# Feed-forward input projections as seven products of quarters

## The chip, the cores and the metric

One core of one Trainium2 chip runs the kernel in one launch. The metric is the device time of an execution in microseconds (us). TensorE is called PE here, VectorE DVE, ScalarE ACT, GpSimd POOL and SyncE, which issues the transfers, SP.

## The reference

The input is 512 tokens of 1024 features, held as `h`. Two blocks follow one another, each of two layers. The change is in the first block's feed-forward, which runs twice in each of its two layers, four times in all:

```python
def swiglu_ffn(x, w_in, w_out):
    gate, up = jnp.split(x @ w_in, 2, axis=-1)
    return (jax.nn.silu(gate) * up) @ w_out
...
h = h + 0.5 * swiglu_ffn(rms_norm(h, ffn1_norm[l]), ffn1_w_in[l], ffn1_w_out[l])
```

`w_in` is 1024 x 5632 (2816 gate and 2816 up columns) and `w_out` 2816 x 1024. The rest of a layer (a mixer of two kinds of heads, attention to a memory of 256 rows) and the second block's layers stay as they are.

## The kernel before

Everything is kept with features on the 128 partitions and tokens along the free axis: `h` is eight tiles of 128 features x 512 tokens. Products are in float32 precision made from two rounded parts: each operand is split into `hi` (a cast on ACT) and `lo` (source minus `hi`, a subtraction on DVE), and `mm3` issues three matmuls for each product: hi by hi, hi by lo, lo by hi.

`weights` (line 239) brings a block of weights in half blocks of up to four 128-row slices of 256 columns: a transfer from SP's queue into `wr`, a cast on ACT into `wh` (line 254), a subtraction on DVE into `wl` (line 255), two buffers of each. `block_fm_steps` (line 271) multiplies one block of 256 columns: for each half block, for each of its two 128-column halves, for each 128-row slice, three matmuls with the weights stationary and 512 tokens moving. `dense_fm_steps` (line 305) does so for a list of blocks and hands each result of 128 x 512 to a function. Both can be advanced a few matmuls at a time.

The feed-forward, `ffn` (line 459), makes the two parts of the normalised input first (`norm`): `xh`, `xl` are parts of `h` times the gain, and the factor of each token, `R`, is multiplied in after the product. It goes through 22 blocks of 128 gate and 128 up columns in groups of 8, 8 and 6 (`FF_GROUPS`). Each block is two times 8 x 3 = 24 matmuls; its results go through DVE and ACT (`gg`, `ss`, `uu`, lines 471 to 474) and are split into `ah`, `al`. After a group its share of the output projection follows, in four blocks of 256 columns that are added to `h` at line 478. There are seven PSUM banks for products.

A planner settles the order of each engine's instructions before the run, by their place in the code; `high_priority(offset=n)` moves what is in it n instructions ahead in that order. Weights have a lead of 80 (`AHEAD`). On the chip each engine takes its instructions in the order so settled, and waits at each for what it needs.

Of the kernel before, what the change touches and what calls it, by code (L numbers as in the profile page):

```python
# [9 lines left out]
F32 = mybir.dt.float32  # L10
F32R = mybir.dt.float32r
I32 = mybir.dt.int32
BF16 = mybir.dt.bfloat16
AF = mybir.ActivationFunctionType
ALU = mybir.AluOpType
# [3 lines left out]
P = 128  # L19
D = 1024  # L20
S = 512
# [1 line left out]
MEM = 256  # L23
DEPTH = 2
FF = 2816
NFF = FF // P
FF_GROUPS = ((0, 8), (8, 16), (16, 22))
NEG = -1e30
GD = 128
XH = 4  # L30
# [76 lines left out]
def _chunks(w, cols):  # L107

    w = np.asarray(w)
    k = w.shape[0] // P  # L110
    return [np.ascontiguousarray(w[:, c].reshape(k, P, -1).transpose(1, 0, 2)).reshape(P, -1) for c in cols]


def _weights(a):

    r256 = lambda lo, hi: [np.arange(c, c + 256) for c in range(lo, hi, 256)]
    out = {}
    for l in range(DEPTH):
        for n in ("ffn1", "ffn2"):
            wi = a[n + "_w_in"][l]  # L120
            wo = a[n + "_w_out"][l]
            out[n + "_in", l] = _chunks(wi, [np.concatenate([np.arange(P) + P * j, np.arange(P) + P * j + FF]) for j in range(NFF)])
            blocks = []
            for lo, hi in FF_GROUPS:
                blocks += _chunks(wo[lo * P : hi * P], r256(0, D))
            out[n + "_out", l] = blocks
        wi = a["w_in"][l]
        z0, a0 = 3072, 3584
        za = [
            np.concatenate([np.arange(z0, z0 + 256), np.arange(a0, a0 + 4)]),  # L130
            np.concatenate([np.arange(z0 + 256, z0 + 512), np.arange(a0 + 4, a0 + 8)]),
        ]
        out["mix_z", l] = _chunks(wi, za)
        out["mix_gdn", l] = _chunks(wi, r256(1536, 3072))
        out["mix_qk", l] = _chunks(wi, r256(0, 1024))
        out["mix_v", l] = _chunks(wi, r256(1024, 1536))
        wo = a["w_out"][l]
        out["mix_out_g", l] = _chunks(wo[4 * P :], r256(0, D))
        out["mix_out_s", l] = _chunks(wo[: 4 * P], r256(0, D))
        out["x_k", l] = _chunks(a["xattn_w_kv"][l], r256(0, D))  # L140
        out["x_v", l] = _chunks(a["xattn_w_kv"][l], r256(D, 2 * D))
        out["x_q", l] = _chunks(a["xattn_w_q"][l], r256(0, D))
        out["x_o", l] = _chunks(a["xattn_w_o"][l], r256(0, D))
        wi = a["w_in_2"][l]
        f0, q0 = 2048, 2056
        qf = [
            np.concatenate([np.arange(q0, q0 + 256), np.arange(f0, f0 + 4)]),
            np.concatenate([np.arange(q0 + 256, q0 + 512), np.arange(f0 + 4, f0 + 8)]),
        ]
        out["s_qf", l] = _chunks(wi, qf)  # L150
        out["s_kb", l] = _chunks(wi, r256(2568, 3080))
        out["s_vb", l] = _chunks(wi, r256(3080, 3592))
        out["s_gb", l] = _chunks(wi, r256(3592, 4104))
        out["s_qa", l] = _chunks(wi, r256(0, 512))
        out["s_ka", l] = _chunks(wi, r256(512, 1024))
        out["s_va", l] = _chunks(wi, r256(1024, 1536))
        out["s_ga", l] = _chunks(wi, r256(1536, 2048))
        out["s_out_b", l] = _chunks(a["w_out_2"][l][4 * P :], r256(0, D))
        out["s_out_a", l] = _chunks(a["w_out_2"][l][: 4 * P], r256(0, D))
        out["s_ple", l] = _chunks(a["w_ple_2"][l], r256(0, D))  # L160
        out["s_gate", l] = _chunks(a["w_ple_gate_2"][l], r256(0, D))
    return out


class Builder:
    def __init__(self, ctx, tc, gain_cols, waps):
        self.tc, self.nc = tc, tc.nc
        self.ctx = ctx
        self.gc = gain_cols
        self.waps = waps  # L170
        pool = lambda name, bufs=1, **kw: ctx.enter_context(tc.tile_pool(name=name, bufs=bufs, **kw))
        self.cp = pool("const")
        self.hp = pool("h")
        self.xp = pool("x")
        self.wp = pool("w")
        self.sp = pool("small", bufs=4)
        self.dp = pool("dram", space=bass.MemoryType.DRAM)
        self.n = self.blocks = 0
        self.pending = []
        self.turn = False  # L180
        self.turn_bank = 'n'
# [52 lines left out]
    def g(self, name, l):  # L234
        lo, hi = self.gc[name, l]
        return self.gt[:, lo:hi]
# [194 lines left out]
    def parts(self, h, gain):  # L431

        xh = self.xp.tile([P, 8, S], F32R, name=self.uid("xh"), tag="xh")
        xl = self.xp.tile([P, 8, S], F32R, name=self.uid("xl"), tag="xl")
        for k in range(8):
            self.split(xh[:, k], xl[:, k], h[k], gain[:, k : k + 1])
        return xh, xl
# [21 lines left out]
    def ffn(self, h, l, name):  # L459
        nc = self.nc  # L460
        with self.scope(self.uid("ffn")) as ap, self.banks(d=7, n=1):
            xh, xl, rc, R = self.norm(h, self.g(name + "_norm", l))
            for gi, (lo, hi) in enumerate(FF_GROUPS):
                n = hi - lo
                ah = ap.tile([P, 8, S], F32R, name=self.uid("ah"), tag="ah", bufs=2)
                al = ap.tile([P, 8, S], F32R, name=self.uid("al"), tag="al", bufs=2)
                for j in range(lo, hi):
                    pg, pu = self.block_fm(name + "_in", l, j, 8, xh, xl)
                    t = lambda s, b=2: ap.tile([P, S], F32, name=self.uid(s), tag=s, bufs=b)
                    gg, ss, uu = t("gg"), t("ss"), t("uu")  # L470
                    nc.vector.tensor_tensor(out=gg, in0=pg, in1=R, op=ALU.mult)  # L471
                    nc.scalar.activation(out=ss, in_=gg, func=AF.Silu)  # L472
                    nc.vector.tensor_tensor(out=uu, in0=pu, in1=R, op=ALU.mult)  # L473
                    nc.vector.tensor_tensor(out=uu, in0=uu, in1=ss, op=ALU.mult)
                    self.split(ah[:, j - lo], al[:, j - lo], uu)

                def add(f, ps):
                    nc.vector.scalar_tensor_tensor(out=h[f % 8], in0=ps, scalar=0.5, in1=h[f % 8], op0=ALU.mult, op1=ALU.add)

                self.dense_fm(name + "_out", l, n, ah, al, add, chunks=range(4 * gi, 4 * gi + 4))  # L480
                if self.mem_c is None and gi == 1:
                    self.memory_stats(lambda shape, tag, bufs: ap.tile(shape, F32, name=self.uid(tag), tag=tag, bufs=bufs))

    def add_to(self, h):
        def add(f, ps):
# [964 lines left out]
def lay(a):  # L1450

    arrays = {"consts": _CONST, "gains": _lay_gains(a)}
    fm = lambda v: np.ascontiguousarray(np.asarray(v).T.reshape(-1, P, v.shape[0]).transpose(1, 0, 2)).reshape(P, -1)
    arrays["xT"] = fm(a["x"][0])
    arrays["memT"] = fm(a["mem"][0])
    for l in range(DEPTH):
        arrays[f"pT{l}"] = fm(a["p_2"][l, 0])
    arrays["pos"] = np.ascontiguousarray(np.asarray(a["positions_2"])[0].reshape(NT, P).T)
    index, flat = {}, {}
    for (name, l), blocks in _weights(a).items():  # L1460
        where = []
        for blk in blocks:
            rows = flat.setdefault(name, [])
            where.append((sum(r.size for r in rows), blk.shape[1]))
            rows.append(blk.reshape(-1))
        index[name, l] = where
    for name, rows in flat.items():
        arrays["w_" + name] = np.concatenate(rows)
    return arrays, index
# [26 lines left out]
```

## Time and profile before

| | |
|---|---|
| median of 3 runs | 3278.52 us (3275.07 to 3278.74) |
| the profiled execution | 3277.66 us, its span 3275.9 us |
| PE busy | 3223.6 us, 98% of the span |
| DVE busy | 1874.4 us, 57% |
| ACT busy | 1307.1 us, 40% |
| transfers | 88 GB/s on average |

The span runs from the first to the last instruction of the trace; the time of the execution has a little around it. An engine's busy time is the sum over its instructions with overlaps counted once. Matmuls overlap one another, so that the duration of one is longer than the distance from one to the next.

### The profile page before, as it was taken

To read this page: it belongs to the slowest core of one execution; us is meant where nothing else is said; L and a number is where in the kernel's file an instruction comes from. 1 tells how busy PE (TensorE), PEld (TensorE's weight loads), DVE (VectorE), ACT (ScalarE), POOL (GpSimd) and SP (SyncE) were. 2 spreads that over 40 slices of the span, in tenths; PEclk is the share of its full clock that TensorE was granted. 3 is DMA by queue.
4 is the path that set the end of the run, shared out by engine and by line. 5 is a ranking of instruction groups with operands and counts; after the bars stand their busy time and mean duration, and the time that the engine had idled before them with its cause. 6 is when DMAs were issued, how large, how long until landed. Compare 5 with 4: busy or idle time off the path is not lost. (4 is left out here: it accounts for less than half of the span.)

```text
span 3275.9 us, 44469 instructions
## 1 busy us (share of the span) xinstructions
PE 3223.6 (98%) x17928; PEld 2652.3 (81%) x17928; DVE 1874.4 (57%) x3404; ACT 1307.1 (40%) x2083; POOL 134.0 (4%) x182
## 2 busy tenths in 40 slices
PE   9999999989999999999999989999999999999999
PEld 7888877778888888888887868888888997789877
DVE  5344567776544435443557776553435667766675
ACT  4222442444432223222353255432223556545563
POOL 0000003220000000000001130000000000000000
PEclk9999999999999999999999999999999999999999
DMA  4323320323222233323321223223223322223223
GB/s 145 97 93 94 91 84 27 84 67 120 67 94 91 96 95 92 97 91 96 90 91 46 65 71 116 65 90 97 92 95 97 91 86 77 78 91 97 71 72 103
DMA packets 84397, 286.92 MB, mean 88 GB/s; under 512 B 9824, under 2 KB 13152, under 8 KB 84192
## 3 DMA queue, kind: packets, MB, share of 16 engines
q1 hardware_dynamic: 84192, 284.10, 28.3%
q8 instruction: 140, 2.29, 0.3%
q14 instruction: 65, 0.53, 0.1%
HBM read 269.38 MB, written 2.10 MB: 83 GB/s over the span
## 5 line engine op out<-in xcount | busy, mean ns | idle before, releaser
L255 DVE TENSOR_TENSOR wl<-wr,wh 128x1024 fp32r<-128x1024 f32 (+2 forms) x512 | 617.2, 1205 | 610.6 <-ACT wh L254 609.2
L254 ACT CAST wh<-wr 128x1024 fp32r<-128x1024 f32 (+2 forms) x512 | 526.9, 1029 | 1002.8 <-PE psd L261 914.1
L261 PE MATMUL psd<-xh,wh 128*128 128x512 f32 x2112 | 842.4, 399 | 8.1 <-ACT xh L384 8.1
L261 PE MATMUL psd<-xl,wh 128*128 128x512 f32 x2112 | 841.5, 398 | 0.0
L261 PE MATMUL psd<-xh,wl 128*128 128x512 f32 x2112 | 838.7, 397 | 0.0
L261 PEld LDWEIGHTS psd<-xh,wh 128*128 128x128 f32 x2112 | 397.2, 188 | 107.8 <-ACT xh L384 8.1
L261 PEld LDWEIGHTS psd<-xh,wl 128*128 128x128 f32 x2112 | 398.1, 188 | 93.5 <-issue 1.2
L261 PEld LDWEIGHTS psd<-xl,wh 128*128 128x128 f32 x2112 | 398.0, 188 | 90.5 <-DVE xl L385 0.3
L261 PE MATMUL psd<-wh,xh 128*128 128x256 f32 (+1 forms) x1024 | 291.7, 285 | 0.1
L261 PE MATMUL psd<-wh,xl 128*128 128x256 f32 (+1 forms) x1024 | 289.5, 283 | 1.2 <-DVE xl L385 1.1
L261 PE MATMUL psd<-wl,xh 128*128 128x256 f32 (+1 forms) x1024 | 288.7, 282 | 0.0
L261 PE MATMUL psd<-ah,wh 128*128 128x512 f32 x704 | 278.3, 395 | 0.0
L261 PE MATMUL psd<-ah,wl 128*128 128x512 f32 x704 | 277.6, 394 | 0.0
L261 PE MATMUL psd<-al,wh 128*128 128x512 f32 x704 | 277.4, 394 | 0.0
L261 PEld LDWEIGHTS psd<-wh,xl 128*128 128x128 f32 x1024 | 193.6, 189 | 1.6 <-DVE xl L385 1.6
L261 PEld LDWEIGHTS psd<-wh,xh 128*128 128x128 f32 x1024 | 193.8, 189 | 1.3 <-ACT xh L384 0.5
L261 PEld LDWEIGHTS psd<-wl,xh 128*128 128x128 f32 x1024 | 194.0, 190 | 0.9
L473 DVE TENSOR_TENSOR uu<-psd,R 128x512 f32<-128x512 f32 x88 | 60.8, 691 | 174.6 <-PE psd L261 174.6
L261 PEld LDWEIGHTS psd<-ah,wl 128*128 128x128 f32 x704 | 131.9, 187 | 32.6
L261 PEld LDWEIGHTS psd<-al,wh 128*128 128x128 f32 x704 | 132.0, 187 | 31.8
L261 PEld LDWEIGHTS psd<-ah,wh 128*128 128x128 f32 x704 | 132.0, 188 | 31.6
L472 ACT ACTIVATE ss<-gg 128x512 f32<-128x512 f32 x88 | 55.8, 634 | 222.9 <-DVE gg L471 222.9
(402 smaller groups left out, 4263.8 us busy)
## 6 DMA issues: line engine op xcount, KB each, us to landing
wr<-w_ffn_in_dram SPq DMA_DIRECT2D x176, 512.0 KB, 3.7
wr<-w_ffn_out_dram SPq DMA_DIRECT2D x64, 512.0 KB, 3.7
wr<-w_ffn_out_dram SPq DMA_DIRECT2D x32, 384.0 KB, 3.1
wr<-w_mix_gdn_dram SPq DMA_DIRECT2D x24, 512.0 KB, 3.8
B<-B SPq DMA_DIRECT2D x40, 256.0 KB, 3.0
wr<-w_mix_qk_dram SPq DMA_DIRECT2D x16, 512.0 KB, 3.8
wr<-w_x_k_dram SPq DMA_DIRECT2D x16, 512.0 KB, 3.8
wr<-w_x_v_dram SPq DMA_DIRECT2D x16, 512.0 KB, 3.8
```

Of the source, the lines that this page charges most:

```text
L254: nc.scalar.copy(hi, raw)
L255: (nc.gpsimd if name in ON_POOL else nc.vector).tensor_sub(lo, raw, hi.bitcast(F32))
L261: mm = lambda a, b, first, last: nc.tensor.matmul(ps, a, b, start=first, stop=last, skip_group_check=flip)
L472: nc.scalar.activation(out=ss, in_=gg, func=AF.Silu)
L473: nc.vector.tensor_tensor(out=uu, in0=pu, in1=R, op=ALU.mult)
```

## The change

The gate and up columns are taken in 11 units of 256 gate and 256 up columns, in groups of 3, 3, 3 and 2. The first two units of a stage are computed as before, gate block and up block after one another (`ffn_plain`). For the others (`ffn_seven_steps`) the tokens are halved (256 each), the 1024 input features are halved (four slices of 128 each), and the columns are gate and up: a product of 2 x 2 by 2 x 2 quarters, made of seven products instead of eight. Sums of the token quarters (`s1` to `s4`) are made once a stage (`seven_parts`), the last in the place of a quarter of `xh`, `xl` that is not needed any more. Sums of the weight quarters are made for every unit, and each of the seven weight operands is split into parts. A product is 2 x 4 x 3 = 24 matmuls of 256 columns. Products accumulate in four banks, two of them more than once after their first content was read; DVE combines them. Loads, sums and splits of a unit's weights are given a lead of 110.

The output blocks of a group, which followed it, are now advanced a step (3, 6 or 9 matmuls) after each product of the next group and two after every fourth; what is left is done at the end of that group, and the last group's blocks at the end.

```diff
--- before.py
+++ after.py
@@ -23,8 +23,11 @@
 MEM = 256
 DEPTH = 2
 FF = 2816
-NFF = FF // P
-FF_GROUPS = ((0, 8), (8, 16), (16, 22))
+HS = S // 2
+FF_UNITS = FF // 256
+FF_GROUPS = ((0, 3), (3, 6), (6, 9), (9, 11))
+FF_PLAIN = 2
+FF_AHEAD = 110
 NEG = -1e30
 GD = 128
 XH = 4
@@ -119,10 +122,10 @@
         for n in ("ffn1", "ffn2"):
             wi = a[n + "_w_in"][l]
             wo = a[n + "_w_out"][l]
-            out[n + "_in", l] = _chunks(wi, [np.concatenate([np.arange(P) + P * j, np.arange(P) + P * j + FF]) for j in range(NFF)])
+            out[n + "_in", l] = _chunks(wi, [256 * u + c + np.arange(256) for u in range(FF_UNITS) for c in (0, FF)])
             blocks = []
             for lo, hi in FF_GROUPS:
-                blocks += _chunks(wo[lo * P : hi * P], r256(0, D))
+                blocks += _chunks(wo[lo * 256 : hi * 256], r256(0, D))
             out[n + "_out", l] = blocks
         wi = a["w_in"][l]
         z0, a0 = 3072, 3584
@@ -162,6 +165,16 @@
     return out
 
 
+class Units:
+
+    def __init__(self, tiles):
+        self.tiles = tiles
+
+    def __getitem__(self, key):
+        return self.tiles[key[1] // 2][:, key[1] % 2]
+
 class Builder:
     def __init__(self, ctx, tc, gain_cols, waps):
         self.tc, self.nc = tc, tc.nc
@@ -459,27 +472,174 @@
     def ffn(self, h, l, name):
         nc = self.nc
         with self.scope(self.uid("ffn")) as ap, self.banks(d=7, n=1):
-            xh, xl, rc, R = self.norm(h, self.g(name + "_norm", l))
+            gain = self.g(name + "_norm", l)
+            xh, xl, rc, R = self.norm(h, gain)
+            t = lambda s, b=2: ap.tile([P, S], F32, name=self.uid(s), tag=s, bufs=b)
+            acts = {}
+            out, late = iter(()), None
+
+            def add(f, ps):
+                nc.vector.scalar_tensor_tensor(out=h[f % 8], in0=ps, scalar=0.5, in1=h[f % 8], op0=ALU.mult, op1=ALU.add)
+
             for gi, (lo, hi) in enumerate(FF_GROUPS):
-                n = hi - lo
-                ah = ap.tile([P, 8, S], F32R, name=self.uid("ah"), tag="ah", bufs=2)
-                al = ap.tile([P, 8, S], F32R, name=self.uid("al"), tag="al", bufs=2)
-                for j in range(lo, hi):
-                    pg, pu = self.block_fm(name + "_in", l, j, 8, xh, xl)
-                    t = lambda s, b=2: ap.tile([P, S], F32, name=self.uid(s), tag=s, bufs=b)
-                    gg, ss, uu = t("gg"), t("ss"), t("uu")
-                    nc.vector.tensor_tensor(out=gg, in0=pg, in1=R, op=ALU.mult)
-                    nc.scalar.activation(out=ss, in_=gg, func=AF.Silu)
-                    nc.vector.tensor_tensor(out=uu, in0=pu, in1=R, op=ALU.mult)
-                    nc.vector.tensor_tensor(out=uu, in0=uu, in1=ss, op=ALU.mult)
-                    self.split(ah[:, j - lo], al[:, j - lo], uu)
-
-                def add(f, ps):
-                    nc.vector.scalar_tensor_tensor(out=h[f % 8], in0=ps, scalar=0.5, in1=h[f % 8], op0=ALU.mult, op1=ALU.add)
-
-                self.dense_fm(name + "_out", l, n, ah, al, add, chunks=range(4 * gi, 4 * gi + 4))
+                turn = 0
+                for u in range(lo, hi):
+                    acts[u] = [ap.tile([P, 2, S], F32R, name=self.uid(s), tag=s, bufs=5) for s in ("ah", "al")]
+                    if u < FF_PLAIN:
+                        self.ffn_plain(name, l, u, xh, xl, R, t, acts[u])
+                        if u == 0:
+                            sums, late = self.seven_parts(ap, h, gain, xh, xl)
+                    else:
+                        if late:
+                            late()
+                            late = None
+                        for _ in self.ffn_seven_steps(name, l, u, ap, xh, xl, sums, R, t, acts[u]):
+                            turn += 1
+                            for _ in range(1 + (turn % 4 == 0)):
+                                next(out, None)
+                self.drain(out)
+                ah, al = (Units([acts[u][i] for u in range(lo, hi)]) for i in range(2))
+                out = self.dense_fm_steps(name + "_out", l, 2 * (hi - lo), ah, al, add, chunks=range(4 * gi, 4 * gi + 4))
                 if self.mem_c is None and gi == 1:
-                    self.memory_stats(lambda shape, tag, bufs: ap.tile(shape, F32, name=self.uid(tag), tag=tag, bufs=bufs))
+                    self.memory_stats(lambda shape, tag, bufs: ap.tile(shape, F32, name=self.uid(tag), tag="ss", bufs=2))
+            self.drain(out)
+
+    def ffn_plain(self, name, l, u, xh, xl, R, t, act):
+
+        nc = self.nc
+        ss = []
+        for ps in self.block_fm(name + "_in", l, 2 * u, 8, xh, xl):
+            gg = t("gg")
+            nc.vector.tensor_tensor(out=gg, in0=ps, in1=R, op=ALU.mult)
+            ss.append(t("ss"))
+            nc.scalar.activation(out=ss[-1], in_=gg, func=AF.Silu)
+        for i, ps in enumerate(self.block_fm(name + "_in", l, 2 * u + 1, 8, xh, xl)):
+            uu = t("uu")
+            nc.vector.tensor_tensor(out=uu, in0=ps, in1=R, op=ALU.mult)
+            nc.vector.tensor_tensor(out=uu, in0=uu, in1=ss[i], op=ALU.mult)
+            self.split(act[0][:, i], act[1][:, i], uu)
+
+    def seven_parts(self, ap, h, gain, xh, xl):
+
+        nc = self.nc
+        lo, hi = slice(0, HS), slice(HS, S)
+        T = lambda: ap.tile([P, 4, HS], F32, name=self.uid("sr"), tag="sr", bufs=6)
+        g = lambda k: gain[:, k : k + 1]
+        part = lambda s: [ap.tile([P, 4, HS], F32R, name=self.uid(s + i), tag=s + i) for i in "hl"]
+        s3, s1, q, s4 = T(), T(), T(), T()
+        stt = lambda o, a, k, op, b: nc.vector.scalar_tensor_tensor(out=o, in0=a, scalar=g(k), in1=b, op0=ALU.mult, op1=op)
+        for k in range(4):
+            nc.scalar.activation(out=s3[:, k], in_=h[k][:, hi], func=AF.Copy, scale=g(k))
+            nc.scalar.activation(out=s4[:, k], in_=h[k + 4][:, lo], func=AF.Copy, scale=g(k + 4))
+            stt(s1[:, k], h[k + 4][:, hi], k + 4, ALU.subtract, s3[:, k])
+            stt(q[:, k], h[k][:, lo], k, ALU.add, s1[:, k])
+            stt(s3[:, k], h[k][:, lo], k, ALU.subtract, s3[:, k])
+        out = {n: part(n) for n in ("s1", "s2", "s3")}
+        self.split(*out["s2"], q, -1.0)
+        self.split(*out["s3"], s3)
+        self.split(*out["s1"], s1)
+        nc.vector.tensor_tensor(out=s4, in0=q, in1=s4, op=ALU.subtract)
+        out["s4"] = [x[:, 0:4, hi] for x in (xh, xl)]
+        return out, lambda: self.split(*out["s4"], s4)
+
+    def ffn_seven_steps(self, name, l, u, ap, xh, xl, s, R, t, act):
+
+        nc = self.nc
+        toks = slice(0, HS), slice(HS, S)
+        A = lambda th, kh: [x[:, 4 * kh : 4 * kh + 4, toks[th]] for x in (xh, xl)]
+        ahead = lambda: self.tc.high_priority(offset=FF_AHEAD)
+        T = lambda: ap.tile([P, 4, 256], F32, name=self.uid("sr"), tag="sr", bufs=6)
+        v = lambda x: x.rearrange("p (j c) -> p j c", j=2)
+        Rh = [R[:, ts].unsqueeze(1).to_broadcast([P, 2, HS]) for ts in toks]
+        tt = lambda o, a, b, op=ALU.add: nc.vector.tensor_tensor(out=o, in0=a, in1=b, op=op)
+
+        def load(c, kh):
+            w = T()
+            nc.sync.dma_start(out=w, in_=self.waps(name + "_in", l, 2 * u + c).rearrange("p (k c) -> p k c", k=8)[:, 4 * kh : 4 * kh + 4])
+            return w
+
+        def parts(w):
+            x = [ap.tile([P, 4, 256], F32R, name=self.uid(n), tag=n, bufs=2) for n in ("sh", "sl")]
+            self.split(*x, w)
+            return x
+
+        def product(ps, w, x, first=True):
+            for j in range(2):
+                fs = slice(j * P, (j + 1) * P)
+                for k in range(4):
+                    start = first and j == 0 and k == 0
+                    for i, (a, b) in enumerate(((0, 0), (0, 1), (1, 0))):
+                        nc.tensor.matmul(ps[:, j], w[a][:, k, fs], x[b][:, k], start=start and i == 0, stop=k == 3 and i == 2, skip_group_check=True)
+
+        xt = lambda tag: v(self.xp.tile([P, S], F32, name=self.uid(tag), tag=tag, bufs=1))
+        a, b, c, d = (self.ps("d", [P, 2, HS]) for _ in range(4))
+        with ahead():
+            b11 = load(0, 0)
+            w = parts(b11)
+        product(a, w, A(0, 0))
+        m1 = xt("acc")
+        nc.scalar.copy(m1, a)
+        yield
+        with ahead():
+            b12 = load(1, 0)
+            p1 = T()
+            tt(p1, b11, b12)
+            b22 = load(1, 1)
+            p2 = T()
+            tt(p2, p1, b22)
+            w = parts(p2)
+        product(b, w, s["s2"])
+        V = xt("sq")
+        tt(V, m1, b)
+        yield
+        with ahead():
+            tt(b12, b12, b22)
+            w = parts(b12)
+        product(c, w, s["s3"])
+        x22 = v(t("uu"))
+        tt(x22, V, c)
+        yield
+        with ahead():
+            w = parts(p1)
+        product(d, w, s["s1"])
+        tt(x22, x22, d)
+        tt(x22, x22, Rh[1], ALU.mult)
+        yield
+        with ahead():
+            b21 = load(0, 1)
+            w = parts(b21)
+        product(a, w, A(0, 1), False)
+        gates = v(t("gg")), v(t("gg"))
+        ss = [v(t("ss")) for _ in range(2)]
+        tt(gates[0], a, Rh[0], ALU.mult)
+        nc.scalar.activation(out=ss[0], in_=gates[0], func=AF.Silu)
+        yield
+        with ahead():
+            tt(p2, p2, b21)
+            w = parts(p2)
+        product(c, w, A(1, 1), False)
+        tt(gates[1], V, c)
+        tt(gates[1], gates[1], Rh[1], ALU.mult)
+        nc.scalar.activation(out=ss[1], in_=gates[1], func=AF.Silu)
+        yield
+        with ahead():
+            w = parts(b22)
+        product(d, w, s["s4"], False)
+        x12 = v(t("uu"))
+        tt(x12, V, d)
+        tt(x12, x12, Rh[0], ALU.mult)
+        for th, x in ((1, x22), (0, x12)):
+            nc.vector.scalar_tensor_tensor(out=x, in0=x, scalar=-1.0, in1=ss[th], op0=ALU.mult, op1=ALU.mult)
+            self.split(*(y[:, :, toks[th]] for y in act), x)
+        yield
 
     def add_to(self, h):
         def add(f, ps):
```

## Rows read from the trace of the kernel before

**Rows 1.** The page's busy times by engine and, in 40 slices, PE's busy share and granted clock.
```profile
PE 3223.6 (98%) x17928; PEld 2652.3 (81%) x17928; DVE 1874.4 (57%) x3404; ACT 1307.1 (40%) x2083; POOL 134.0 (4%) x182
...
PEclk9999999999999999999999999999999999999999
```
**Rows 2.** PE's waits over the whole span: us in total, times, longest.
```profile
PE pst L923 <- DVE sbr L375: 20.9, 8, 3.6
PE psd L261 <- ACT xh L384: 8.1, 1, 8.1
```
**Rows 3.** Busy time by engine from 9 to 346 us, with clock and DMA share.
```profile
core 0: us, PE busy (x) PEld busy (x) DVE busy (x) ACT busy (x) POOL busy (x), PEclk, DMA share, GB/s
9.00:346.00 337.00, 337.00 (x1451) 271.57 (x1451) 155.01 (x214) 101.70 (x126) 0.00 (x0) 1.00 0.33 102
```
**Rows 4.** DVE's timeline inside the input projections: start us, duration us, instruction, idle before.
```profile
199.78 0.69 DVE L471 TENSOR_TENSOR gg<-psd,R 128x512 f32<-128x512 f32 x1 [0.68 <-PE psd L261]
202.57 0.69 DVE L473 TENSOR_TENSOR uu<-psd,R 128x512 f32<-128x512 f32 x1 [2.10 <-PE psd L261]
203.37 0.69 DVE L474 TENSOR_TENSOR uu<-uu,ss 128x512 f32<-128x512 f32 x1
203.97 1.22 DVE L255 TENSOR_TENSOR wl<-wr,wh 128x1024 fp32r<-128x1024 f32 x1
205.11 0.69 DVE L382 TENSOR_TENSOR al<-uu,ah 128x512 fp32r<-128x512 f32 x1
209.07 1.22 DVE L255 TENSOR_TENSOR wl<-wr,wh 128x1024 fp32r<-128x1024 f32 x1 [3.28 <-ACT wh L254]
210.97 0.69 DVE L471 TENSOR_TENSOR gg<-psd,R 128x512 f32<-128x512 f32 x1 [0.68 <-PE psd L261]
```
**Rows 5.** ACT's groups from 100 to 340 us: busy us, mean ns, idle before and releaser.
```profile
L254 ACT CAST wh<-wr 128x1024 fp32r<-128x1024 f32 x43 | 45.1, 1050 | 133.6 <-PE psd L261 133.6
```
**Rows 6.** 256-wide matmuls of a later stage on PE's timeline, and their weight loads.
```profile
2580.80 0.28 PE L261 MATMUL psd<-wh,xh 128*128 128x256 f32 x1
...
2583.51 0.28 PE L261 MATMUL psd<-wh,xl 128*128 128x256 f32 x1
...
2584.87 0.28 PE L261 MATMUL psd<-wh,xh 128*128 128x256 f32 x1
...
2588.96 0.28 PE L261 MATMUL psd<-wl,xh 128*128 128x256 f32 x1
...
L261 PEld LDWEIGHTS psd<-wh,xl 128*128 128x128 f32 x1024 | 193.6, 189 | 1.6 <-DVE xl L385 1.6
```
**Rows 7.** Groups of equal shape over the span, as in rows 5.
```profile
L255 DVE TENSOR_TENSOR wl<-wr,wh 128x1024 fp32r<-128x1024 f32 x456 | 561.2, 1231 | 568.4 <-ACT wh L254 567.1
L254 ACT CAST wh<-wr 128x1024 fp32r<-128x1024 f32 x456 | 478.3, 1049 | 939.2 <-PE psd L261 859.4 <-issue 53.9 <-DMA wr<-w_x_v_dram 15.5
L478 DVE SCALAR_TENSOR_TENSOR h<-psd,h 128x512 f32<-128x512 f32 x96 | 66.3, 690 | 94.7 <-PE psd L261 94.7
L385 DVE SCALAR_TENSOR_TENSOR xl<-h,gains,xh 128x512 fp32r<-128x512 f32 x88 | 64.2, 750 | 21.0 <-ACT xh L384 20.8
L474 DVE TENSOR_TENSOR uu<-uu,ss 128x512 f32<-128x512 f32 x88 | 60.9, 692 | 9.1 <-ACT wh L254 0.5 <-ACT ss L472 0.2
L472 ACT ACTIVATE ss<-gg 128x512 f32<-128x512 f32 x88 | 55.8, 634 | 222.9 <-DVE gg L471 222.9
L255 DVE TENSOR_TENSOR wl<-wr,wh 128x768 fp32r<-128x768 f32 x32 | 30.6, 956 | 24.7 <-ACT wh L254 24.7
...
39.25 0.42 DVE L406 TENSOR_TENSOR acc<-acc,sq 128x256 f32<-128x256 f32 x1
```
**Rows 8.** Weight transfers (KB each, us to landing), and SP's waits from 100 to 344 us.
```profile
wr<-w_ffn_in_dram SPq DMA_DIRECT2D x176, 512.0 KB, 3.7
wr<-w_ffn_out_dram SPq DMA_DIRECT2D x64, 512.0 KB, 3.7
...
SPq L253 <- DVE wl L255: 219.4, 42, 6.2
```

## Prediction

> **What bounds the kernel now.** I began with the engines' busy shares: TensorE (PE) 98%, VectorE (DVE) 57%, ScalarE (ACT) 40%, the granted clock at its full level throughout [rows 1]. A busy PE need not be a PE at its best pace, so the waits come next. PE is not busy for 3275.9 - 3223.6 = 52 us in all; of its waits the largest group lies outside the feed-forward stages, and the next, 8.1 us, is the very start [rows 2]. From 9 to 346 us, which is the first feed-forward stage, PE is busy 337.00 of 337.00 us while DVE has 155 and ACT 102 [rows 3]. So this stage is bound by the number of PE steps, and by nothing else: whatever the change takes from PE's steps is won, until another engine makes PE wait.
>
> The pace of a step is start to start, not the duration shown, for matmuls overlap. In the projections DVE meets the same instruction (`gg`, line 471) every 210.97 - 199.78 = 11.19 us [rows 4]. The code puts 48 matmuls of 512 columns between them, so one takes 0.2331 us. In the same rows, two neighbours without a wait show DVE's pace: 0.60 us from a 512-wide operation to the next, 1.14 us after a 1024-wide one. The cast of the next weights waits for PE, 133.6 us over 43 casts [rows 5]: it waits for PE to let go of the buffer. That is the loop that will matter: product ends, cast, subtraction, next product but one.
>
> **What is removed and added on PE.** A unit of 256 gate and 256 up columns is two old blocks, 96 matmuls of 512 columns: 96 x 0.2331 = 22.38 us. In the new form it is seven products of 2 x 4 x 3 = 24 matmuls of 256 columns, 168 in all. 256-wide matmuls stand elsewhere in the trace: 23 steps from 2580.80 to 2583.51 us make 0.1178 us, 34 steps from 2584.87 to 2588.96 make 0.1203 [rows 6]. I take the middle, 0.119: 168 x 0.119 = 19.99 us. So one eighth of the columns goes, but 2% comes back through the narrower step. A unit wins 2.39 us (2.59 and 2.17 at the two bounds). Units 0 and 1 of each stage stay plain, nine change, in four stages: 36 x 2.39 = 86 us (93 to 78). The output projection keeps its 528 matmuls a stage, in four groups instead of three.
>
> **What is added on DVE and ACT.** Durations are those of [rows 7]. Per changed unit DVE gets four sums and seven `lo` subtractions of 1024, and thirteen 512-wide operations on the products (six that read PSUM to combine or scale, three more scalings by R, two multiplications by the Silu, two `lo`). By mean durations that is 11 x 1.231 + 13 x 0.69 = 22.5 us; by the paces above 11 x 1.14 + 13 x 0.60 = 20.3. Two old blocks cost 4 x 1.231 + 8 x 0.69 = 10.4. ACT gets seven casts at 1.05, a copy, two Silu and two casts at about 0.63: 10.5 us, never the limit.
>
> Whether this is hidden depends on the place. In the second and third group of units the previous group's output blocks lie between the products: 4 x 36 x 0.2331 = 33.6 us of PE to three units, 11.2 each, 1.6 per product. They bring DVE eight 768-wide subtractions and eight additions, (8 x 0.956 + 8 x 0.69) / 3 = 4.4 us a unit. PE then has 31.2 us a unit and DVE at most 26.9, 86%. The last group's two units get 17 of 24 output steps, much the same; the rest follows after. So DVE's work fits, but it comes in lumps: after the seventh product six operations (4.1 us) stand together with the next unit's sums. I charge 0.5 us for each of 8 x 4 filled units, 16 us. The bounds are 0 (all of it waits in the gaps) and the slow rival below.
>
> Unit 2 has no output blocks beside it. PE needs 20.0 us; DVE 20.3 to 22.5 and a last split of 1.2. Before it, the two plain units hold PE for 44.8 us, and DVE has the norm (8 x 0.75 + 7 x 0.69 = 10.8), the plain units (20.9) and the new sums of token quarters (twelve 256-wide at about 0.42, four subtractions and sums of about 1.23: 10): 42 us, so no slack is carried in. DVE is the limit there, by 1.5 to 3.7 us; evictions can be put off into unit 3, where PE has slack, which would make it 0. A product takes 24 x 0.119 = 2.86 us, and a double-buffered pair of parts needs 1.05 + 1.23 = 2.3 us after the product before last ends: it fits, with half a microsecond to spare for a DVE that is busy all the time. I take 3 us a stage, 12 in all (0 to 7 each).
>
> **Transfers, queues, banks.** A stage loads the same 11 x 4 half blocks of input weights of 512 KB as before and 28 instead of 24 output blocks, the same bytes; one lands in 3.7 us, and the DMA share of the stage is 0.33 [rows 3, 8]. POOL has no part in it. All go through SP's queue, which already waits 219 us in the stage for DVE to release a buffer, without PE noticing. A unit's six f32 tiles now turn over in six slots, so a load of the next unit (`b22`) can hold up SP until the sixth product's parts are made; behind it stand the output weights. They have a turn or two of 4.5 us against 3.7, so I cost this at nothing; without that cover it is some 3 us a unit. Four product banks and two output banks fit in seven. The eight more additions to `h` per stage fall to DVE in the gaps. In the first stage the statistics of `mem` share two scratch tiles with the products; a few 256-wide operations, at most 3 us, inside the margins.
>
> **The sum.** The profiled execution took 3277.66 us (span 3275.9 and 1.8 around it), 0.9 below the median of the runs. 3277.7 - 86 + 12 + 16 = 3219.7; with the 0.9, 3220 us.
>
> **Rivals.** *All of it hidden.* DVE serves the weight parts first and puts evictions off; then only PE's count tells: 3278.5 - 86 = 3192, 3185 at the quick pace. For it: PE shows not one wait in the stage now [rows 3], and the new work has a lead of 110 instructions. Against: unit 2's sum.
>
> *Slower: the subtraction stands behind an eviction.* DVE works in order. If an eviction of product n+1 is queued ahead of the `lo` of product n+2, that `lo` can start only when n+1 has ended: 0.69 + 1.23 = 1.92 us, against fillers of 3, 6 or 9 matmuls (0.7, 1.4, 2.1 us) or none. After the three sizes that leaves 1.2, 0.5 and 0, some 0.6 on average, and about 0.45 as every fourth turn has two fillers; 56 filled turns a stage and seven unfilled make 25 + 13 = 39 us, 154 in all, 3346 us. It decides from 86 / 252 = 0.34 us per product upward; at 0.37 the kernel is measurably slower. For it: DVE above 85% busy, with work in lumps. Against: the lead of 110 instructions is nearly three turns of about 38, so parts should be queued ahead of evictions, and buffers free when a product ends give the eviction room during the cast.
> [...]
>
> *Slower: weight loads come out.* Seven products need 72 more weight loads a unit, 2592 in all. If a load of 0.188 us were not covered, that is 487 us, 3680 or so. Against it: the 256-wide steps of 0.12 us are shorter than the load of 0.188 us that each needs [rows 6], so loads overlap already.
> [...]
>
> **Chances.** My own case, 3203 to 3237: 0.45. All hidden, below 3203: 0.20. More lost than I charge, 3237 to 3272: 0.11. Nothing measurable, within 0.2% (6.6 us, what a measurement of this kernel can tell from no change): 0.05. Slower through DVE's order: 0.18; through weight loads: 0.01. So faster 0.76, same 0.05, slower 0.19. The range of 3187 to 3285 takes in the first four cases almost whole and leaves out the slower ones.
>
> **What would show it.** Right: 256-wide matmuls at 0.118 to 0.120 us; about 2592 more matmuls; DVE near 85% in the stages; PE's waits for a `lo` split or cast in unit 2 of each stage and few elsewhere; a feed-forward stage some 14 to 17 us shorter. Wrong: waits of PE for DVE in every turn (slow rival), none (hidden), a 256-wide pace above 0.133 us (no gain at all), or a granted clock that falls to its lower level in the gaps, which nothing here shows and which I leave out of the sum.

## The result, and the profile after

The changed kernel takes 3199.27 us (3195.22 to 3199.73, 4 runs) against 3277.24 us before: a ratio of 0.976, 95% interval 0.9743 to 0.9777, 78 us less. The profiled execution took 3195.22 us (span 3192.9), the quickest of the four; against the 3277.66 us of before's that is 82.4 us less. 3220 us was forecast, with 3187 to 3285 as the range. The time lies between the forecast and the rival in which all new work is hidden (3192 us); by the prediction's own bounds it is that rival's case (below 3203 us, chance 0.20) and not its main one (3203 to 3237 us, 0.45).

The page's busy times, to be held against [rows 1]:

```profile
PE 3134.1 (98%) x20520; PEld 2718.9 (85%) x20520; DVE 2326.2 (73%) x3952; ACT 1451.7 (45%) x2291; POOL 133.8 (4%) x182
...
PEclk9999999999999999999999999999999999999999
```

PE has 20520 - 17928 = 2592 matmuls more and is busy 89.5 us less. DVE got 452 us of work and lies at 73%. The waits of PE, us in total, times and longest, against [rows 2]:

```profile
PE pst L1083 <- DVE sbr L388: 20.8, 8, 3.5
PE psd L274 <- ACT xh L397: 7.2, 1, 7.2
PE psd L580 <- DVE sl L395: 5.2, 8, 1.8
...
PE psd L274 <- ACT wh L267: 0.9, 1, 0.9
```

Line 580 is the matmul of the seven products and line 395 its `lo` subtraction. For 6048 matmuls PE waited eight times, 5.2 us in all, and every one of these waits lies in unit 2 of a stage. In the second and third group of the first stage, where output blocks stand between the products, PE never waits although DVE is busy 84% of the time:

```profile
core 0: us, PE busy (x) PEld busy (x) DVE busy (x) ACT busy (x) POOL busy (x), PEclk, DMA share, GB/s
57.00:80.00 23.00, 22.48 (x186) 21.99 (x185) 19.38 (x23) 10.40 (x13) 0.00 (x0) 1.00 0.40 126
...
112.00:210.00 98.00, 98.00 (x684) 91.09 (x684) 82.21 (x116) 42.38 (x56) 0.00 (x0) 1.00 0.34 108
```

The first row is unit 2, the second lies in the filled groups. From start to start, 1456 steps between 256-wide matmuls of the first stage average 0.1182 us; two more hold a wait.

**Where the time went.** A stage ends with the last `xl` split of the norm behind it. The first stage lies between these splits, before:

```profile
12.55 1.42 DVE L385 SCALAR_TENSOR_TENSOR xl<-h,gains,xh 128x512 fp32r<-128x512 f32 x2
385.63 0.75 DVE L385 SCALAR_TENSOR_TENSOR xl<-h,gains,xh 128x512 fp32r<-128x512 f32 x1 [0.51 <-ACT xh L384]
```

and after:

```profile
12.17 1.41 DVE L398 SCALAR_TENSOR_TENSOR xl<-h,gains,xh 128x512 fp32r<-128x512 f32 x2
363.70 0.75 DVE L398 SCALAR_TENSOR_TENSOR xl<-h,gains,xh 128x512 fp32r<-128x512 f32 x1 [0.89 <-ACT xh L397]
```

From the end of one such split to the end of the next, the four stages took 372.4, 371.5, 371.7 and 371.1 us before and 350.9, 350.4, 351.4 and 348.8 after: 21.5, 21.1, 20.3 and 22.3 us less, 85.3 in all before rounding. The steps account for it: 22.38 - 168 x 0.1182 = 2.52 us a unit, 36 units, 90.8 us; less the waits of 5.2 us that is 85.6. The rest of the program took 2.3 us longer in this pair of executions.

### The profile page after: what moved, and what is told of

Read it like the earlier page. It is cut to its first block, busy times and chain, and to the rows that moved or that the text cites. A ratio compares the mean times of both kernels' runs of the same rounds, so it can differ in the third digit from the quotient of the medians.

```text
span 3192.9 us, 50423 instructions
## 1 busy us (share of the span) xinstructions
PE 3134.1 (98%) x20520; PEld 2718.9 (85%) x20520; DVE 2326.2 (73%) x3952; ACT 1451.7 (45%) x2291; POOL 133.8 (4%) x182
## 5 line engine op out<-in xcount | busy, mean ns | idle before, releaser
L268 DVE TENSOR_TENSOR wl<-wr,wh 128x1024 fp32r<-128x1024 f32 (+3 forms) x384 | 443.1, 1154 | 211.4 <-ACT wh L267 209.4
L267 ACT CAST wh<-wr 128x1024 fp32r<-128x1024 f32 (+3 forms) x384 | 378.1, 985 | 399.4 <-PE psd L274 285.9
L394 ACT CAST sh<-sr 128x1024 fp32r<-128x1024 f32 x252 | 264.8, 1051 | 503.7 <-PE psd L580 474.4
L274 PE MATMUL psd<-xh,wh 128*128 128x512 f32 x960 | 387.0, 403 | 7.2 <-ACT xh L397 7.2
L274 PE MATMUL psd<-xl,wh 128*128 128x512 f32 x960 | 385.5, 402 | 0.2 <-DVE xl L398 0.2
L274 PE MATMUL psd<-xh,wl 128*128 128x512 f32 x960 | 384.9, 401 | 0.2 <-DVE wl L268 0.2
L580 PE MATMUL psd<-xh,sl 128*128 128x256 f32 x1152 | 322.7, 280 | 5.2 <-DVE sl L395 5.2
L580 PE MATMUL psd<-xh,sh 128*128 128x256 f32 x1152 | 322.5, 280 | 0.0
L580 PE MATMUL psd<-xl,sh 128*128 128x256 f32 x1152 | 321.9, 279 | 0.0
L395 DVE TENSOR_TENSOR sl<-sr,sh 128x1024 fp32r<-128x1024 f32 x252 | 307.3, 1220 | 15.1 <-ACT sh L394 14.2
```

The lines of the kernel that those rows point to most:

```text
L267: nc.scalar.copy(hi, raw)
L268: (nc.gpsimd if name in ON_POOL else nc.vector).tensor_sub(lo, raw, hi.bitcast(F32))
L274: mm = lambda a, b, first, last: nc.tensor.matmul(ps, a, b, start=first, stop=last, skip_group_check=flip)
L394: nc.scalar.copy(hi, src)
L395: nc.vector.tensor_tensor(out=lo, in0=src, in1=hi.bitcast(F32), op=ALU.subtract)
L580: nc.tensor.matmul(ps[:, j], w[a][:, k, fs], x[b][:, k], start=start and i == 0, stop=k == 3 and i == 2, skip_group_check=True)
```

## The experiments

**All units plain.** `FF_PLAIN` is 11; the groups, the order and the loads are those of the change.

```diff
-FF_PLAIN = 2
+FF_PLAIN = 11
...
-                        if u == 0:
+                        if u == 0 and FF_PLAIN < FF_UNITS:
```

> All eleven units of a stage are plain blocks; only the groups of 3, 3, 3 and 2, the order gate block before up block and the loads are those of the change (no sums of token quarters are made). Theory (the gain is the eighth of the 512-wide columns that PE no longer streams, nothing else): no gain, 3277 us within 7. Rival (part of the gain is the regrouping, which shortens the last output blocks and the tail of a stage): 10 to 30 us below before.

3280.83 us, ratio 1.0011 (1.0001 to 1.0020). The regrouping brings nothing, and costs 3 us if anything; what is won is won by the seven products.

**Eight narrow products.** In the kernel before, every matmul of the input projections is cut into two of 256 tokens.

```diff
-                    self.mm3(ps, wh[:, k, fs], wl[:, k, fs], xh[:, kk], xl[:, kk], kk == 0, kk == kt - 1)
+                    if name in ("ffn1_in", "ffn2_in"):
+                        for i in range(2):
+                            ts = slice(256 * i, 256 * i + 256)
+                            for g, (a, b) in enumerate(((wh, xh), (wh, xl), (wl, xh))):
+                                nc.tensor.matmul(ps[:, ts], a[:, k, fs], b[:, kk, ts], start=kk == 0 and i == 0 and g == 0, stop=kk == kt - 1 and g == 2, skip_group_check=True)
...
```

> The kernel before, with every matmul of the input projections cut into two of 256 tokens, each with its own weight load: eight products, so to say. Theory (a 256-wide step is 0.118 us against half of 0.233): 88 blocks x (96 x 0.118 - 48 x 0.2331) = 12 us more than before, 3289 us. Rival (weight loads of 0.188 us come partly uncovered, or instructions cannot be fetched fast enough): 3310 us or more.

3285.43 us, ratio 1.0026 (1.0014 to 1.0037): 7.5 us for 4224 more matmuls and weight loads. Its 256-wide steps are 0.1175 us (1311 of them, from 100 to 345 us), and 88 x (96 x 0.1175 - 48 x 0.2331) = 8 us. The weight loads stay covered.

**Output blocks after the group.** Seven products, nothing between them.

```diff
-                            for _ in range(1 + (turn % 4 == 0)):
-                                next(out, None)
-                self.drain(out)
                 ah, al = (Units([acts[u][i] for u in range(lo, hi)]) for i in range(2))
                 out = self.dense_fm_steps(name + "_out", l, 2 * (hi - lo), ah, al, add, chunks=range(4 * gi, 4 * gi + 4))
+                self.drain(out)
```

> Seven products as in the change, but a group's output blocks follow the group instead of lying between the next group's products. Theory (DVE needs 20.3 us or more for a unit that PE does in 19.9, so the output blocks between are what hides it): PE waits for the split in nearly every unit, 1 to 3 us each for 36 units, 3235 to 3300 us. Rival (the lead and the buffers carry DVE's lumps over, the place of the output blocks is no matter): within 10 us of the changed kernel's 3199.

3226.06 us, ratio 0.9842 (0.9827 to 0.9857): 27 us slower than the change, under my 36 us at least and over the rival's 10. So the filler is worth about a third of the gain. The waits for the split:

```profile
PE psd L578 <- DVE sl L395: 17.0, 29, 2.1
```

That is 12 us more than in the change. The steps between 256-wide matmuls of the first stage average 0.1199 us here, with some of 0.22 to 0.43 among them that are too short to be listed as waits; 6048 x 0.0017 = 10 us. DVE alone keeps nearly abreast of PE, at under a microsecond lost for each unit without filler.

**A short lead.** `FF_AHEAD` is 20.

```diff
-FF_AHEAD = 110
+FF_AHEAD = 20
```

> The lead of loads, sums and splits is 20 instructions instead of 110, less than one product. Theory of the prediction's slow rival (with parts queued behind evictions and loads issued late, PE waits some 0.4 us or more per product): 252 products x 0.4 = 100 us more, about 3300 us. Rival (the planner's order follows what is ready, the lead only breaks ties): below 3215 us.

3197.04 us, ratio 0.9757 (0.9743 to 0.9772); PE waits 4.3 us for splits. The lead makes no difference to the time, and next to none to DVE's order: 245 of the 252 weight `lo` subtractions stand behind the same number of product readings as with a lead of 110. So the run doesn't bring about the order that the slow rival feared, and doesn't show what it would cost.

**More work on DVE.** Three of seven, then all seven `lo` subtractions are done twice, between the first one and the product that needs it. The diff is that of the first run; in the second the condition is gone.

```diff
+        done = []
...
             self.split(*x, w)
+            done.append(w)
+            if len(done) % 2 == 0:
+                tt(x[1], w, x[0].bitcast(F32), ALU.subtract)
             return x
```

> The changed kernel with three of a unit's seven lo subtractions done twice: 3 x 1.14 = 3.4 us more on DVE per changed unit, in the way of the product that waits for it. Theory (beside output blocks DVE has 31 us a unit and used some 24 to 25; only unit 2 of a stage, without output blocks, shows it): 2 to 4 us more per stage, 3207 to 3215 us. Rival (the work comes in lumps, so each added subtraction delays its product by half of its length or more): 108 x 0.6 = 65 us more, 3260 us.

3202.08 us, ratio 0.9769 (0.9754 to 0.9783): 3 to 5 us above the two measurements of the change, for 108 x 1.14 = 123 us of added DVE work. Less than I expected.

> All seven lo subtractions of a unit done twice: 8.0 us more on DVE per unit. Theory (DVE then needs 20.3 + 8.0 + 3.9 = 32.2 us at least where PE needs 31.0, and 28.3 against 19.9 in unit 2, so it becomes the limit everywhere): 1.2 to 4 us for each of 32 filled units and 8 for each unit 2, 3270 to 3360 us. Rival (DVE has far more room than its busy time says): below 3240 us.

3242.77 us, ratio 0.9893 (0.9876 to 0.9909): 44 to 46 us more for 252 x 1.14 = 287 us of work; neither theory's number. The filled groups with all doubled:

```profile
112.00:210.00 98.00, 92.72 (x619) 84.87 (x619) 93.09 (x117) 38.04 (x50) 0.00 (x0) 0.97 0.33 103
```

DVE at 95% is the limit now, and PE idles 5.3 of 98 us. About five sixths of what was added was still hidden.

**Token sums in slots of their own.** In unit 2 of the second stage the changed kernel's DVE timeline reads (start, duration, idle before):

```profile
930.71 1.23 DVE L395 TENSOR_TENSOR sl<-sr,sh 128x1024 fp32r<-128x1024 f32 x1 [0.26 <-ACT sh L394]
...
933.47 1.22 DVE L395 TENSOR_TENSOR sl<-sr,sh 128x1024 fp32r<-128x1024 f32 x1 [0.20 <-ACT sh L394]
937.16 1.23 DVE L562 TENSOR_TENSOR sr<-sr,sr 128x1024 f32<-128x1024 f32 x1 [2.47 <-DMA sr<-w_ffn_in_dram]
938.30 0.68 DVE L562 TENSOR_TENSOR uu<-sq,psd 128x512 f32<-128x512 f32 x1
938.90 1.22 DVE L395 TENSOR_TENSOR sl<-sr,sh 128x1024 fp32r<-128x1024 f32 x1
```

DVE stands idle for 2.47 us until a weight quarter lands, and the split behind it is the one that PE's timeline shows it waiting for:

```profile
940.17 0.38 PE L580 MATMUL psd<-xh,sl 128*128 128x256 f32 x1 [1.71 <-DVE sl L395]
```

SP's queue issued the load that DVE waits for only at 931.97 us:

```profile
924.17 0.33 SPq L566 DMA_DIRECT2D sr<-w_ffn_in_dram  x1
928.50 0.33 SPq L266 DMA_DIRECT2D wr<-w_ffn_out_dram  x1
931.97 16.99 SPq L566 DMA_DIRECT2D sr<-w_ffn_in_dram  x4
```

It had waited 3.1 us for the subtraction of 930.71 to let go of a slot; of SP's waits from 925 to 932 us:

```profile
SPq L566 <- DVE sl L395: 3.1, 1, 3.1
```

Counted through in order, this load and the sum at 937.16 belong to unit 3: the four loads of unit 2 were issued by 900.19 us and its four sums begun by 909.41, before PE came to it at 926.63. So a sum of the next unit stands ahead of a subtraction of this one in DVE's order and waits for its transfer, while the cast that the subtraction needs is done by 936.31:

```profile
935.26 1.05 ACT L394 CAST sh<-sr 128x1024 fp32r<-128x1024 f32 x1 [1.83 <-PE psd L580]
```

In all eight waits of PE the subtraction stands like this, behind a sum of unit 3. As the reason for the late transfer I took the token sums, which hold four of the six slots at the opening of a stage. The edit puts them elsewhere.

```diff
-        T = lambda: ap.tile([P, 4, HS], F32, name=self.uid("sr"), tag="sr", bufs=6)
+        T = lambda tag: ap.tile([P, 4, HS], F32, name=self.uid("st"), tag=tag, bufs=5)
...
-        s3, s1, q, s4 = T(), T(), T(), T()
+        s3, s1, q, s4 = T("ah"), T("al"), T("ah"), T("al")
```

> The changed kernel with the temporaries of the token sums in four slots of the activations' tags, which are free at the start of a stage, instead of four of the six slots that unit 2's weights need. Theory (PE's 5 us of waits in unit 2 come from weight transfers that are issued late because those slots are taken): PE's waits for the split fall below 1.5 us in all and the time by 3 to 6 us, 3193 to 3197 us. Rival (the waits come from DVE's pace, 20.3 us a unit against 19.9): waits and time as before this edit, 3199 us within 2.

3194.64 us, ratio 0.9748 (0.9733 to 0.9762). The waits fell from 5.2 to 2.5 us, not below 1.5. To see whether the time differs it ran again, beside the change itself:

> The changed kernel once more, beside the next run on the same chip: 3197 to 3200 us.

> The token sums in slots of their own once more. If earlier transfers are worth what PE's waits for the split showed (5.2 us against 2.5), 2 to 4 us below the changed kernel of the same call. If the earlier difference of 4.6 us was the spread between calls, no difference.

The change took 3197.12 us (ratio 0.9756, 0.9743 to 0.9769) with 4.7 us of waits, the edit 3196.47 (0.9750, 0.9737 to 0.9764) with 3.1. The edit takes a third to a half of the waits away; in the time the two can't be told apart. What is left has the same cause, so the slots of the token sums were only a part of it. In the second stage of the last run SP, DVE and PE show:

```profile
932.28 0.33 SPq L566 DMA_DIRECT2D sr<-w_ffn_in_dram  x1
```

```profile
931.03 1.22 DVE L395 TENSOR_TENSOR sl<-sr,sh 128x1024 fp32r<-128x1024 f32 x1 [0.26 <-ACT sh L394]
...
937.26 1.23 DVE L562 TENSOR_TENSOR sr<-sr,sr 128x1024 f32<-128x1024 f32 x1 [1.18 <-DMA sr<-w_ffn_in_dram]
938.40 1.22 DVE L395 TENSOR_TENSOR sl<-sr,sh 128x1024 fp32r<-128x1024 f32 x1
```

```profile
939.68 0.39 PE L580 MATMUL psd<-xh,sl 128*128 128x256 f32 x1 [1.21 <-DVE sl L395]
```

The load again waits for unit 2's own subtraction to free a slot. More slots, or the sum of the next unit further back in DVE's order, were not tried.

**One plain unit.** With the token sums in their own slots as above.

```diff
-FF_PLAIN = 2
+FF_PLAIN = 1
```

> As the run with the token sums in slots of their own, and only unit 0 of a stage plain. PE loses another 4 x 2.54 = 10 us of steps. Theory (at the opening of a stage DVE has the norm, a plain unit, the token sums and two changed units, 73 us, against 62 us of PE): PE waits 3 to 10 us more a stage, 3195 to 3225 us, so no gain. Rival (with transfers in time and evictions put off the opening is hidden): 3184 to 3188 us.

3231.20 us, ratio 0.9859 (0.9844 to 0.9873): 35 to 37 us slower than the two measurements with two plain units, 6 us beyond the range that I expected, and not by waits for weight splits (2.3 us). PE's waits are headed by one that the change does not have:

```profile
PE psd L580 <- ACT s2h L397: 32.3, 4, 10.5
```

The busy times around the first of them, with the granted clock behind POOL's:

```profile
30.00:40.00 10.00, 7.61 (x49) 6.66 (x47) 8.37 (x22) 5.26 (x8) 0.00 (x0) 1.00 0.27 79
40.00:50.00 10.00, 1.50 (x3) 0.91 (x4) 10.00 (x19) 7.28 (x14) 0.00 (x0) 0.52 0.16 52
50.00:60.00 10.00, 10.00 (x70) 10.00 (x70) 7.87 (x8) 3.14 (x3) 0.00 (x0) 0.80 0.00 0
```

In each stage PE waits 6 to 10 us for the token sum `s2`, once, and here the granted clock falls to its lower level: 0.52 and 0.80 of the upper one on average in the two slices around the gap. The waits of 32.3 us less the 10 us of steps explain the larger part of the loss; the lower clock is part of the rest, 70 matmuls in the last row where 0.118 us a step would make 85. In the change, the second plain unit is what covers the making of the token sums.

**Token sums first.** One plain unit again, with the sums ahead of it in the code.

```diff
                         self.ffn_plain(name, l, u, xh, xl, R, t, acts[u])
-                        if u == 0:
-                            sums, late = self.seven_parts(ap, h, gain, xh, xl)
...
+                        if u == 0:
+                            sums, late = self.seven_parts(ap, h, gain, xh, xl)
                         self.ffn_plain(name, l, u, xh, xl, R, t, acts[u])
```

> One plain unit, and the token sums stand before it in the code instead of behind it (with slots of their own). Theory (what cost 32 us with one plain unit was only the place of the token sums, which stood behind the plain unit's evictions on DVE): the 6 to 10 us gaps go, PE loses 10 us of steps and waits 1 to 5 us a stage for splits, 3186 to 3202 us. Rival (DVE's 73 us of work at the opening against 62 of PE is the limit): gaps of 5 us or more a stage remain, 3205 us or more.

3197.48 us, ratio 0.9754 (0.9741 to 0.9768), as expected by the theory: the place of the sums was the fault. But it is no quicker than the change either. The 10 us of steps are given back in part at the very start of the program:

```profile
PE psd L274 <- ACT wh L267: 14.4, 1, 14.4
```

PE's first matmul waits 14.4 us for the cast of the first weights, against 7.2 us for `xh` in the change. From split to split of the norms the second and third stage are 2.7 and 2.3 us shorter than with two plain units (346.9 and 347.6 us against 349.6 and 349.9), as the steps would have it, but the first is 6.7 us longer and the fourth 1.7. At the opening of the fourth PE waits for weights too:

```profile
PE psd L274 <- DVE wl L268: 2.4, 1, 2.4
```

A version that puts the sums first in the last three stages alone was not tried.

**Two weight sums on POOL.** As the last run, with `p1` and the sum of `b12` and `b22` made on POOL.

```diff
-            tt(p1, b11, b12)
+            nc.gpsimd.tensor_tensor(out=p1, in0=b11, in1=b12, op=ALU.add)
...
-            tt(b12, b12, b22)
+            nc.gpsimd.tensor_tensor(out=b12, in0=b12, in1=b22, op=ALU.add)
```

> As the run with the token sums first, and two of a unit's four weight sums on POOL, which takes about 2.5 us for each by its 512-wide rows of 1.28 us; DVE loses 2.3 us a unit. Theory (DVE is short only at the opening): 0 to 5 us less than with the sums on DVE. Rival (the longer sum, in the way of the second and third product, makes PE wait): slower than that by 5 us or more.

3254.02 us, ratio 0.9931 (0.9917 to 0.9944), 57 us slower than with the sums on DVE; the reason, as far as it was followed, is in the last section.

## Why the prediction was right, and where its sizes were off

The mechanism of the gain held: the stage was bound by PE's steps, an eighth of the columns of nine units went, and most of that was won. What the prediction charged against it was too much. In the filled units all of DVE's new work was hidden, as its rival "all of it hidden" had it, and the time came out in that rival's band. That the range took it in is owed to its width: 3187 to 3285 us was drawn to hold four of the cases, that rival among them. Term by term:

- *Steps saved:* 86 us forecast at 0.119 us a step; the step was 0.1182 and the saving 90.8. "About 2592 more matmuls" was exact, "a feed-forward stage some 14 to 17 us shorter" was too little: 20 to 22.
- *Filled units, 16 us:* the mis-sized term. No wait is listed there, so the true charge is about 0. DVE was at 84% against the 86% I worked out, so its load was about right; that load in lumps costs something was argued, and neither the change nor the doubled subtractions show it. Three added subtractions a unit cost 3 to 5 us in all.
- *Unit 2, 12 us:* PE waited 5.2 us there. The place was right and the cause was not the one named. I had DVE's pace as the limit, with no slack carried in. The trace shows slack carried in: in the second stage the last of the unit's four sums was begun 17 us before PE came to the unit, and in the window of unit 2 above DVE is busy 19.38 of 23 us. The waits begin with a load of unit 3 that lands late and a sum of unit 3 that stands ahead of unit 2's subtraction. I had seen that loads of `sr` queue for slots, and priced it at nothing because the turns of output blocks cover it; unit 2 has no such turns, and I did not ask there. Freeing the token sums' slots left 2.5 and 3.1 us of waits, by the same chain.
- *Transfers otherwise, banks, the last group:* next to nothing listed, as costed.
- *DVE's order as slow rival:* the order that it supposed did not come about. In the trace of the change four of the 252 weight subtractions stand behind the reading of the product just before theirs, and with a lead of 20 four again. So my argument against it, that the lead puts parts ahead of evictions, was not the reason, and what such an order would cost was not measured. What held PE up in unit 2 was another wrong order, a sum of the next unit ahead of the subtraction. That DVE works in order, which the rival supposed, these rows show: the cast was done by 936.31 us, yet DVE, idle until 937.16, began the sum first and the subtraction at 938.90.
- *Weight loads as slow rival:* it fell, by 7.5 us for 4224 added loads.
- *One row was misread:* "From 9 to 346 us, which is the first feed-forward stage" takes in only most of it; by the norm behind it the stage ends near 385 us. The argument didn't need the end.

The sum: forecast 86 - 28 = 58 us; with the measured step and the waits for splits 90.8 - 5.2 = 85.6, of which the medians of the runs show 78 and the profiled pair 82.4. The last few microseconds lie between stages and in the spread of single executions, and were not traced further.

## What to carry to other kernels

Where a stage shows PE busy without a gap, work out what a change takes from its steps, start to start, and then ask only where another engine would make it wait; an engine at 84% need not, if its work for the next product but one can go ahead. Filling matmuls of another kind between products are worth their place when the other engine is close to PE's pace, here 27 of some 80 us. Look at the opening of a stage by itself: the place of one-time sums decides there, 34 us with one plain unit. Ask of work that is done ahead whether what it waits for can come late: on an engine that works in order it holds up what stands behind it, here all of the 5.2 us.

## What was not expected of the hardware

A sum on POOL held up an operation of DVE's by 2.1 us. With two weight sums on POOL, POOL's timeline reads:

```profile
84.00 2.40 POOL L594 TENSOR_TENSOR sr<-sr,sr 128x1024 f32<-128x1024 f32 x1 [16.50 <-DMA sr<-w_ffn_in_dram]
91.20 3.44 POOL L604 TENSOR_TENSOR sr<-sr,sr 128x1024 f32<-128x1024 f32 x1 [4.80 <-DMA sr<-w_ffn_in_dram]
```

DVE's at the same time:

```profile
84.13 3.35 DVE L395 TENSOR_TENSOR sl<-sr,sh 128x1024 fp32r<-128x1024 f32 x1
88.72 1.22 DVE L395 TENSOR_TENSOR sl<-sr,sh 128x1024 fp32r<-128x1024 f32 x1
91.18 1.23 DVE L562 TENSOR_TENSOR sr<-sr,sr 128x1024 f32<-128x1024 f32 x1
92.33 3.39 DVE L395 TENSOR_TENSOR sl<-sr,sh 128x1024 fp32r<-128x1024 f32 x1
```

And PE's:

```profile
87.53 0.38 PE L580 MATMUL psd<-xh,sl 128*128 128x256 f32 x1 [1.53 <-DVE sl L395]
95.77 0.38 PE L580 MATMUL psd<-xh,sl 128*128 128x256 f32 x1 [2.37 <-DVE sl L395]
```

A subtraction that takes 1.22 us alone took 3.35 us when POOL's sum of 2.40 us had begun 0.13 us before it; it ended at 87.48 us, 1.08 us after that sum. At 91.18 it was DVE that began first, and POOL's sum took 3.44 us, 1.04 us more than the other. So in these rows, of two operations that each read two operands from SBUF, one waited for the other; by what, they do not show. An operation of DVE's that reads one of its operands from PSUM was not held: the 44 of 512 columns that began during such a sum took 0.67 to 0.69 us, as elsewhere. One of them, behind POOL's row:

```profile
141.59 2.40 POOL L594 TENSOR_TENSOR sr<-sr,sr 128x1024 f32<-128x1024 f32 x1 [22.02 <-DMA sr<-w_ffn_in_dram]
```

```profile
143.06 0.69 DVE L562 TENSOR_TENSOR uu<-sq,psd 128x512 f32<-128x512 f32 x1 [2.44 <-PE psd L580]
```

In the whole run DVE is rid of 80 sums of 1.22 us, 98 us, and its 280 weight subtractions and 80 remaining sums take 52 us longer in all (means of 1.35 and 1.42 us against 1.22). PE waited for splits 28.3 us in 17 waits; in 12 of them, 23.7 us, the split itself took 2.6 to 3.4 us. Of the rest of the 57 us some lies in longer waits at the openings of the stages and in the clock (0.987 of the upper level on average against 0.994); it was not added up.

The clock was the other thing. In the run with one plain unit a gap of 10.5 us in PE's work came with the lower granted clock, a mean of 0.52 in the ten microseconds of the gap and 0.80 in the next ten; the waits of up to 1.8 us in the changed kernel left it at 1.00. In the traces of before and of the change the lower level is 0.50, and the prediction's "at its full level throughout" was too much: it is granted from 641 to 643 us before and from 620.5 to 623.5 in the change, outside the feed-forward stages and with PE busy 2.00 of 2.00 and 2.99 of 3.00 us. The means over the span are 0.995 and 0.994.
